# Paired products for B and C of two Mamba groups, and an earlier place for convolutions and two output copies

## The chip, the cores and the metric

The kernel runs on one core of a Trainium2 chip. The metric is the device time of one launch in microseconds (us). Engines are named as the profile names them: PE is TensorE's matmul, PEld its weight load, DVE VectorE, ACT ScalarE, POOL GpSimd, SP SyncE, which here only issues loads.

## What is computed

One decoder layer on 512 tokens with 16 learned meta tokens in front (length 528, width 1024), all in float32:

```python
u = rmsnorm(h, mix_norm_w)
proj = u @ w_in           # pool 1024, z 2048, xBC 4096, dt 32, two gates of 1024
xbc = silu(causal_depthwise_conv(xbc, conv_w, conv_b))          # width 4
y = ssd_chunked(x, dt, a, B, C) + x * d_skip    # 8 groups, 4 heads each of 64, state 128, chunks of 128
y = rmsnorm_per_group(y * silu(z)) * ssd_norm_w
y_ssd  = y @ w_ssd_out                           # 2048 -> 1024
y_pool = pool_mixer(proj's pool part) @ w_pool_up
h = h + (sigmoid(g0) * y_pool + sigmoid(g1) * y_ssd) @ w_o
h = h + relu(rmsnorm(h) @ w_ff1) ** 2 @ w_ff2    # hidden width 4096
out = rmsnorm(h)[meta tokens dropped]
```

Each of the eight groups of the state-space part needs a B and a C (128 channels each), an x of 256 channels (two tiles of 128) and a z of 256, all from w_in.

## The kernel before

**Products.** A float32 factor is split into a high and a low fp32r part: ACT casts the raw weight tile to `whi` (L111) and DVE subtracts it to `wlo` (L113). Each product is then three matmuls: high by high, high by low, low by high. `block` loads one weight tile of 128x1024 through SP and splits it with raised priority; `proj` (L215, L218) multiplies it with the eight row tiles of u, `uh` and `ul`.

**Scheduling.** The program is written as Python generators, and a scheduler orders each engine's instructions by dependencies, place in the program and priority. `tc.high_priority(100)` raises an instruction's priority, `tc.issue_after(x)` keeps an instruction behind another. Each engine takes its list in order.

**Scan stage.** For g from 0 to 7, `weave` (called at L933) steps in turn through `ssd(g)`, through `group_proj(g + 1)`, which makes the next group's inputs, and through side work: weight sums on POOL's queue (`weight_sums_at`) and, in the first four groups, sums of u. At g = 4 the first half of the output projection, `out_half` (eight products `pso`), comes ahead of the next group's projections. At g = 7 there is no next group; `out_part` (the products `psp` over the inputs 8 to 13) takes that place.

**`group_proj(g)`** makes B and C first, then x, for groups 2, 3 and 4 a gate (`pgp`), and z last (`pz`). A tile is made in one of two ways. `plain` multiplies one weight block: 48 matmuls in two column halves into a two-bank PSUM tile `px`, which `conv` reads directly. `pair` (L494 to L525) makes two tiles together with seven half-size products in place of eight: the left factors are quarters of the weight or sums of quarters, the right ones u, or sums of u's tiles made in the first four groups. `MULTIPLY` gives their order, b11, b21, t2, t1, s3, b22, t4; each has 12 matmuls of 264 columns. They go to two PSUM banks, `pq` and `po` (the first, third, fifth and seventh to `pq`); after each, the bank is copied by ACT (b11 L511, t2 L516, t1 L518, t4 L525) or added by DVE (b21 L513, s3 L521, b22 L523) into two raw tiles, `ra` and `rb` (`raw_pair`). The conv then reads those. Before the change x is made in this way for groups 4 to 7 (`X_PAIRS`), B and C for none (`BC_PAIRS` is empty). The weight sums are made by POOL's accumulating DMAs: each set of `fx` takes eight copies of 512 KB and serves two pairs; two sets are used before.

**`conv`** is ACT's Identity with scale and bias (L437), three DVE multiply-adds (L440) and ACT's Silu (L442), in the scheduler's ordinary priority.

**`ssd(g)`**: PE transposes B (`ptb`, L606), the meta part (`ptm`) and x (`ptx`, L619); DVE weights x (`xdt`, `xdd`); ACT makes two exponentials `eb` (L633), behind z's silu (L584) from group 4 on, eight Relu steps of the decay `abc` (L638, DVE does the other half at L641), and two exponentials over it (L644, L645). Then PE multiplies C with B (`pcb`, L656), DVE masks it, PE makes the chunks' states (`pst`, L663, L665), DVE passes them from chunk to chunk (L672, L673) and multiplies decay and mask (`dm`, L676). Two steps `po` (L685) and `py` (L691) give y; DVE multiplies it with z (L694 to L698); a norm over the group follows (`png` L709, L710). `filled` holds `pcb` behind the last matmul of the next group's first plain tile, `second_product` holds z's first matmul behind t2 of its group's x pair.

**The end of the scan.** `out_part` first multiplies inputs 8 to 11 for two output tiles (`psp0`, `psp1`), then inputs 12 and 13 for both together, kind of matmul by kind, and then copies both to `sp` (L868), from where POOL adds them into `acc_d` by DMA (L869); the other six output tiles follow. After the scan come the last inputs of the output projection, the pool branch (its products are at L998), gates, w_o and the MLP (lines from L940 on), none of which is edited.

Of the kernel before, what the change touches and what calls it, by code (L numbers as in the profile page):

```python
# [11 lines left out]
AF = mybir.ActivationFunctionType  # L12
ALU = mybir.AluOpType
# [3 lines left out]
SEQ = 512  # L17
# [17 lines left out]
V_MIX, V_BG, V_PS, V_CW, V_CB, V_DS, V_SN, V_MN, V_DTB, V_AL = (  # L35
    0, 8, 24, 32, 160, 192, 208, 224, 232, 233)
# [11 lines left out]
SUMS_AT = range(4)  # L48

X_PAIRS = (4, 5, 6, 7)  # L50
BC_PAIRS = ()
PAIRS = [(k, g) for g in range(G) for k in "bx" if g in (BC_PAIRS if k == "b" else X_PAIRS)]

SETS_AT = {0: 1, 1: 1, 2: 2, 3: 1, 4: 2, 5: 2, 6: 1, 7: 1}
# [10 lines left out]
def kernel(ctx: ExitStack, tc, xT, x, w, fx, f1, f2, vec, fnw, out):  # L65
    nc = tc.nc
    act, dve, pe, pool = nc.scalar, nc.vector, nc.tensor, nc.gpsimd
# [98 lines left out]
    def col(off, i, n=P):  # L166
        return vs[:n, off + i : off + i + 1]
# [25 lines left out]
    def psum2(name):  # L193
        return psa.tile([P, 1024], F32, tag="mm", name=name)
# [239 lines left out]
    def conv(dst, src, ct):  # L434
        n = dst.shape[-1]
        e = src.shape[-1] - n
        act.activation(dst, src[:, e:], AF.Identity, bias=col(V_CB, ct), scale=col(V_CW, ct * 4 + 3))  # L437
        for j in range(1, 4):
            o = max(0, j - e)
            dve.scalar_tensor_tensor(dst[:, o:], src[:, e + o - j : e + n - j],  # L440
                                     col(V_CW, ct * 4 + 3 - j), dst[:, o:], op0=ALU.mult, op1=ALU.add)
        silu = act.activation(dst, dst, AF.Silu)  # L442
        mark[0] = dst[:, :1]
        if ct < 16:
            x_ready[ct // 2] = silu
# [48 lines left out]
    def pair(kind, g, r):  # L494

        banks = (psum2(f"pq{kind}{g}")[:, :HALF], psum1(f"po{kind}{g}")[:, :HALF])
        operands = pair_operands(PAIRS.index((kind, g)))
        one, two = HF
        for m, f, n, start, stop in MULTIPLY:
            o = banks[n]  # L500
            wt = next(operands)
            f = factor_u(f)
            for low in range(2):
                for k in range(4):
                    wk = wt[low][:, k * P : (k + 1) * P]
                    at = pe.matmul(o, wk, f[k][0], start=start and not low and k == 0,  # L506
                                   stop=stop and low == 1 and k == 3, skip_group_check=True)
                    if not low:
                        pe.matmul(o, wk, f[k][1], start=False, stop=False, skip_group_check=True)
            if m == "b11":  # L510
                act.copy(r[0][:, one], o)  # L511
            elif m == "b21":
                dve.tensor_tensor(r[0][:, one], r[0][:, one], o, op=ALU.add)  # L513
            elif m == "t2":
                second_product[g] = at
                act.activation(r[1][:, one], o, AF.Copy, scale=-1.0)  # L516
            elif m == "t1":
                act.copy(r[1][:, two], o)  # L518
                yield
            elif m == "s3":  # L520
                dve.tensor_tensor(r[1][:, two], r[1][:, two], o, op=ALU.subtract)  # L521
            elif m == "b22":
                dve.tensor_tensor(r[1][:, one], r[1][:, one], o, op=ALU.add)  # L523
            else:
                act.copy(r[0][:, two], o)  # L525

    def raw_pair(kind, g):
        return [stg.tile([P, L], F32, tag=t, name=f"{t}{kind}{g}") for t in ("ra", "rb")]

    def group_proj(g, cur, gate=None):  # L530

        first = g == 0
        xc, bt, ct, zt = cur

        def plain(dst, t, skip):
            if first and (dst is bt or dst is ct):
                view = viewB if dst is bt else viewC
            else:
                runs, view = wide(psum2(f"px{g}_{t}"), skip)
                proj(runs, block(), X if first else U)  # L540
            conv(dst, first_raw(t, view, skip) if first else view, t)

        def z_half(ps, i):

            with tc.issue_after(done[0].ins) if g == 1 else nullcontext():
                wt = block(None, halved.get(g - 1) if gate is not None else None)
            proj(narrow(ps), wt, X if first else U, None if i else second_product.get(g))

        bcs = ((bt, 16 + g, 0), (ct, 24 + g, NM - 4))
        xs = ((xc[:, 0, :], 2 * g, 0), (xc[:, 1, :], 2 * g + 1, 0))  # L550
        both = g in BC_PAIRS
        for kind, ts, paired in (("b", bcs, both), ("x", xs, g in X_PAIRS)):
            if paired:
                r = raw_pair(kind, g)
                yield from pair(kind, g, r)
                for (dst, t, skip), src in zip(ts, r):
                    conv(dst, src[:, skip:], t)
                yield
            else:
                for t in ts:  # L560
                    plain(*t)
                    filled.setdefault(g - 1, mm[0])
                    yield
            if both:
                i = 0 if kind == "b" else 1
                ps = psum2(f"pz{g}_{i}")[:, :SEQ]
                z_half(ps, i)
                z_ready[g] = act.activation(zt[:, i, :], ps, AF.Silu)
                yield
        if both:  # L570
            return
        if gate is not None:
            gate_pool(gate)
            yield
        ps = psum2(f"pz{g}")
        for i in range(2):
            z_half(ps[:, i * SEQ : (i + 1) * SEQ], i)
        zf = zt.rearrange("p i t -> p (i t)")
        if first:
            dve.tensor_tensor(zt, ps.rearrange("p (i t) -> p i t", i=2),  # L580
                              rsb[:, NM:].unsqueeze(1).to_broadcast([P, 2, SEQ]), op=ALU.mult)
            z_ready[g] = act.activation(zf, zf, AF.Silu)
        else:
            z_ready[g] = act.activation(zf, ps, AF.Silu)  # L584
        yield
# [253 lines left out]
    def out_part():  # L839

        def get(n):
            t = block_tiles()
            block_load(t, slice(0, 1024))

            with after(b_meta[G - 1] if n == 1 else None):
                cast = act.copy(t[2], t[1])
            if n == 1:
                late_cast[0] = cast
            with tc.issue_after(x_decayed[G - 1].ins) if n == 1 else nullcontext():
                dve.tensor_tensor(t[3], t[1], t[2].bitcast(F32), op=ALU.subtract)  # L850
            return t

        def pieces():
            blocks = [get(0), get(1)]
            for n in range(6):
                t = blocks[n] if n < 2 else get(n)
                for j in range(NK):
                    c = slice(j * P, (j + 1) * P)
                    yield t[2][:, c], t[3][:, c]

        un = pieces()

        def part(ps, d, ks):
            mm3s(ps, [(next(un), ys[k]) for k in ks], ks[0] == 8, ks[-1] == 13)

        def add(ps, d):
            o = staged(f"sp{d}")
            act.copy(o, ps)  # L868
            nc.gpsimd.dma_start(acc_d[d], o, accum_op=ALU.add)  # L869


        ps = [psum2(f"psp{d}")[:, :SEQ] for d in range(2)]
        for d in range(2):
            part(ps[d], d, range(8, 12))
            yield
        late = [[(next(un), ys[k]) for k in (12, 13)] for d in range(2)]
        for o in ((0, 0), (1, 0), (0, 1)):
            for d in range(2):
                for n, (a, b) in enumerate(late[d]):
                    pe.matmul(ps[d], a[o[0]], b[o[1]], start=False, stop=o[1] == 1 and n == 1)  # L880
            yield
        for d in range(2):
            add(ps[d], d)
        for d in range(2, NK):
            ps = psum2(f"psp{d}")[:, :SEQ]
            part(ps, d, range(8, 14))
            add(ps, d)
            yield
# [791 lines left out]
def _weight_blocks(i):  # L1680
# [14 lines left out]

    def group(g, gate_d=None):
        z = lambda j: put(cols(w_in, OFF_Z + (2 * g + j) * P))
        both = g in BC_PAIRS
        for i, ts in enumerate(((16 + g, 24 + g), (2 * g, 2 * g + 1))):
            if g not in (X_PAIRS if i else BC_PAIRS):  # L1700
                for t in ts:
                    put(cols(w_in, OFF_XBC + t * P))
            if both:
                z(i)
        if gate_d is not None:
            gate(gate_d)
        if not both:
            for j in range(2):
                z(j)

    def wg(b):
        put(w_g[2 * b : 2 * b + 2].reshape(2, 2, P, 256).transpose(2, 0, 1, 3).reshape(P, 1024))
# [119 lines left out]
```

## Time and profile before

| | |
|---|---|
| device time, median of 3 runs | 1002.07 us (1002.04 to 1004.28) |
| the profiled execution | 1003.26 us |
| its span | 1001.6 us (1.66 us lie around it) |
| granted TensorE clock, mean | 0.999 |
| instructions | 15673 |
| moved by DMA | 184.52 MB; HBM read 173.13 MB, written 58.59 MB |

The busy times of the engines are shown with the prediction. In the span's 40 slices PE is at 9 tenths or more in all but the last, where it is at 7. The profile's chain that ended last goes over PE for 84%, DVE for 7%, ACT for 4% and DMA for 3%. The costliest groups are PE's matmuls and the two halves of the splits; the share of the loads' 16 DMA engines is 33.3% for SP's queue and 26.4% for POOL's.

A row of a view by time gives the start, the duration, engine, line and what is written from what; `x8` means eight instructions in one row, and what stands in brackets is the idle time ahead of it on its engine and what ended it. All times are in us from the start of the span.

### The profile page before, as it was taken

What the parts mean: (1) busy time and instruction counts of PE and PEld (TensorE: products, weight loads), DVE (VectorE), ACT (ScalarE), POOL (GpSimd) and SP (SyncE); (2) the same over time, 40 slices, a digit from 0 to 9 for tenths busy, and PEclk for the clock granted to TensorE, in tenths of its full rate; (3) what the DMA queues carried; (4) which work ended last, traced back from release to release, by engine and by line L of the source; (5) the groups of instructions that cost most, each with busy time, mean ns of one, the idle gap of its engine ahead of it and who ended that gap; (6) DMA issues with size and microseconds to landing.
All of it is one profiled execution on the core that took longest, in us unless ns stands there. A gap on an engine that the chain in (4) does not pass through costs nothing.

```text
span 1001.6 us, 15673 instructions
## 1 busy us (share of the span) xinstructions
PE 989.0 (99%) x6035; PEld 873.4 (87%) x6035; DVE 804.2 (80%) x1162; ACT 602.9 (60%) x855; POOL 121.9 (12%) x215
## 2 busy tenths in 40 slices
PE   9999999999999999999999999999999999999997
PEld 7889898989889999978898888888889999999986
DVE  7977997879855888978789667876988878888885
ACT  7657749494924658574345443377666666656654
POOL 0010321211212312223200001121000000000000
PEclk9999999999999999999999999999999999999999
DMA  7374868676798849678823732889354464454332
GB/s 245 89 254 140 265 182 238 195 192 199 221 262 265 232 122 278 211 161 172 286 68 127 252 101 77 259 232 323 88 197 149 142 194 138 157 185 151 129 106 84
DMA packets 61803, 184.52 MB, mean 184 GB/s; under 512 B 7072, under 2 KB 8416, under 8 KB 60704
## 3 DMA queue, kind: packets, MB, share of 16 engines
q1 hardware_dynamic: 39456, 109.00, 33.3%
q0 software_dynamic: 18240, 67.51, 26.4%
q10 hardware_dynamic: 4032, 7.00, 1.9%
q8 instruction: 47, 0.77, 0.3%
q14 instruction: 28, 0.23, 0.1%
HBM read 173.13 MB, written 58.59 MB: 231 GB/s over the span
## 4 chain that ended last, share of the span: by engine, by line
PE 84%; DVE 7%; ACT 4%; DMA 3%; issue 1%; SPq 0%; ACTq 0%; DVEq 0%
PE px L1451 8%; PE px L215 7%; PE alpha L1519 6%; PE pz L215 6%; PE px L1454 4%; PE px L218 4%; PE pgp L215 3%; PE alpha L1522 3%; PE pz L218 3%; PE pgs L215 3%; DMA raw<-in_w 2%; PE pqx L506 2%; PE py L691 2%; PE pgp L218 2%; PE pso L146 1%; PE wo_alpha L1213 1%
## 5 line engine op out<-in xcount | busy, mean ns | idle before, releaser
L113 DVE TENSOR_TENSOR wlo<-raw,whi 128x1024 fp32r<-128x1024 f32 (+2 forms) x88 | 102.2, 1171 | 45.0 <-ACT whi L111 29.7
L111 ACT CAST whi<-raw 128x1024 fp32r<-128x1024 f32 (+2 forms) x88 | 87.2, 1012 | 64.0 <-DMA raw<-in_w 15.8
L215 PE MATMUL px<-uh,whi 128*128 128x264 f32 (+1 forms) x320 | 81.1, 291 | 0.0
L218 PE MATMUL px<-ul,whi 128*128 128x264 f32 (+1 forms) x320 | 78.7, 284 | 0.0
L1226 DVE TENSOR_TENSOR ht<-ht,alpha 128x1024 f32<-128x1024 f32 x35 | 42.7, 1220 | 29.1 <-PE alpha L1519 29.1
L215 PEld LDWEIGHTS px<-uh,whi 128*128 128x128 f32 x320 | 60.5, 189 | 1.1 <-issue 0.9
L1149 ACT CAST shi<-rawf 128x1024 fp32r<-128x1024 f32 x42 | 44.2, 1053 | 28.0 <-PE alpha L1522 18.4
L218 PEld LDWEIGHTS px<-ul,whi 128*128 128x128 f32 x320 | 60.2, 188 | 0.4 <-issue 0.2
L1519 PE MATMUL alpha<-shi,hh 128*128 128x512 f32 x140 | 55.3, 395 | 0.7 <-DVE ht L1226 0.6
L1522 PE MATMUL alpha<-shi,hl 128*128 128x512 f32 x140 | 54.7, 391 | 0.0
L1150 DVE TENSOR_TENSOR slo<-rawf,shi 128x1024 fp32r<-128x1024 f32 x42 | 51.2, 1219 | 0.6 <-ACT shi L1149 0.6
L1454 PE MATMUL px<-vsl,shi 128*128 128x256 f32 x192 | 47.4, 280 | 0.0
L1451 PE MATMUL px<-vsh,shi 128*128 128x256 f32 x192 | 47.4, 281 | 0.0
L215 PE MATMUL pz<-uh,whi 128*128 128x512 f32 x112 | 43.8, 391 | 1.7 <-DVE xc L440 1.7
L218 PE MATMUL pz<-ul,whi 128*128 128x512 f32 x112 | 43.6, 390 | 0.0
L215 PE MATMUL px<-uh,wlo 128*128 128x264 f32 (+1 forms) x320 | 42.0, 283 | 0.0
L215 PEld LDWEIGHTS px<-uh,wlo 128*128 128x128 f32 x320 | 40.0, 188 | 0.0
L1519 PE MATMUL alpha<-slo,hh 128*128 128x512 f32 x140 | 37.4, 389 | 0.0
L1451 PEld LDWEIGHTS px<-vsh,shi 128*128 128x128 f32 x192 | 36.2, 188 | 0.9
L1454 PEld LDWEIGHTS px<-vsl,shi 128*128 128x128 f32 x192 | 36.1, 188 | 0.9
L1454 PE MATMUL px<-vl,shi 128*128 128x256 f32 x144 | 36.1, 283 | 0.0
L1451 PE MATMUL px<-vh,shi 128*128 128x256 f32 x144 | 36.0, 282 | 0.0
(599 smaller groups left out, 3068.3 us busy)
## 6 DMA issues: line engine op xcount, KB each, us to landing
raw<-in_w SPq DMA_DIRECT2D x96, 512.0 KB, 4.6
f_t<-in_f POOLq DMA_DIRECT2D x38, 512.0 KB, 7.5
f_s<-in_f POOLq DMA_DIRECT2D x26, 512.0 KB, 7.0
b<-in_f SPq DMA_DIRECT2D x21, 512.0 KB, 4.4
rawf<-in_f SPq DMA_DIRECT2D x36, 256.0 KB, 3.0
rawf<-f_t SPq DMA_DIRECT2D x36, 256.0 KB, 3.1
abc<-acs_d POOLq DMA_DIRECT2D x8, 1024.0 KB, 8.3
f_t<-f_t POOLq DMA_DIRECT2D x12, 512.0 KB, 6.7
```

Of the source, the lines that this page charges most:

```text
L111: act.copy(hi[:, c], raw[:, c])
L113: dve.tensor_tensor(lo[:, c], raw[:, c], hi[:, c].bitcast(F32), op=ALU.subtract)
L215: pe.matmul(o, wt, rhs[0][k][:, c], start=part == 0 and k == 0, stop=part == 1 and k == NK - 1)
L218: mm[0] = pe.matmul(o, wt, rhs[1][k][:, c], start=False, stop=False)
L506: at = pe.matmul(o, wk, f[k][0], start=start and not low and k == 0, stop=stop and low == 1 and k == 3, skip_group_check=True)
L1149: splits.append((act.copy(hi, src), dve.tensor_tensor(lo, src, hi.bitcast(F32), op=ALU.subtract)))
L1150: dve.tensor_tensor(lo, src, hi.bitcast(F32), op=ALU.subtract)))
L1226: added[0] = dve.tensor_tensor(o, o, src, op=op)
L1451: pe.matmul(ps, m, f[k][0], start=start and not low and k == 0, stop=stop and low == 1 and k == 3, skip_group_check=True)
L1454: pe.matmul(ps, m, f[k][1], start=False, stop=False, skip_group_check=True)
L1519: pe.matmul(ps[t], hh[:, p, seg, st], m, start=bool(first and not low and p == 0), stop=bool(last and low and p == 1), skip_group_check=True)
L1522: pe.matmul(ps[t], hl[:, p, seg, st], m, start=False, stop=False, skip_group_check=True)
```

## The change

1. `BC_PAIRS` becomes (5, 6): B and C of groups 5 and 6 are made by `pair` instead of two `plain` tiles. A third set of `fx` sums is made for them. Their raw values are held in the group's own x tile `xc` (128 x 2 x 528), which x's convolution overwrites later, and not in `ra` and `rb`.
2. For these groups z stays one step after x; an older form, in which half of z followed each pair, is taken out, here and in the order of the weight blocks. `filled` is set for them too: `pcb` of the group before stands behind the last matmul of the B and C pair's t2.
3. In `conv` the Identity and the three multiply-adds get raised priority; the Silu does not.
4. In `out_part` the inputs 12 and 13 are multiplied for one output tile after the other, and each tile's copy and its accumulating DMA follow at once with raised priority.

```diff
-BC_PAIRS = ()
+BC_PAIRS = (5, 6)
@@ def conv(dst, src, ct):
-        act.activation(dst, src[:, e:], AF.Identity, bias=col(V_CB, ct), scale=col(V_CW, ct * 4 + 3))
-        for j in range(1, 4):
-            o = max(0, j - e)
-            dve.scalar_tensor_tensor(dst[:, o:], src[:, e + o - j : e + n - j],
-                                     col(V_CW, ct * 4 + 3 - j), dst[:, o:], op0=ALU.mult, op1=ALU.add)
+        with tc.high_priority(100):
+            act.activation(dst, src[:, e:], AF.Identity, bias=col(V_CB, ct), scale=col(V_CW, ct * 4 + 3))
+            for j in range(1, 4):
+                o = max(0, j - e)
+                dve.scalar_tensor_tensor(dst[:, o:], src[:, e + o - j : e + n - j],
+                                         col(V_CW, ct * 4 + 3 - j), dst[:, o:], op0=ALU.mult, op1=ALU.add)
         silu = act.activation(dst, dst, AF.Silu)
@@ def group_proj(g, cur, gate=None):
-        both = g in BC_PAIRS
-        for kind, ts, paired in (("b", bcs, both), ("x", xs, g in X_PAIRS)):
+        for kind, ts, paired in (("b", bcs, g in BC_PAIRS), ("x", xs, g in X_PAIRS)):
             if paired:
-                r = raw_pair(kind, g)
-                yield from pair(kind, g, r)
+                r = raw_pair(kind, g) if kind == "x" else [xc[:, i, :] for i in range(2)]
+                for _ in pair(kind, g, r):
+                    filled.setdefault(g - 1, second_product[g])
+                    yield
                 for (dst, t, skip), src in zip(ts, r):
                     conv(dst, src[:, skip:], t)
                 yield
...
-            if both:
-                i = 0 if kind == "b" else 1
-                ps = psum2(f"pz{g}_{i}")[:, :SEQ]
-                z_half(ps, i)
-                z_ready[g] = act.activation(zt[:, i, :], ps, AF.Silu)
-                yield
-        if both:
-            return
@@ def out_part():
-        for o in ((0, 0), (1, 0), (0, 1)):
-            for d in range(2):
+        for d in range(2):
+            for o in ((0, 0), (1, 0), (0, 1)):
                 for n, (a, b) in enumerate(late[d]):
                     pe.matmul(ps[d], a[o[0]], b[o[1]], start=False, stop=o[1] == 1 and n == 1)
+            with tc.high_priority(100):
+                add(ps[d], d)
             yield
-        for d in range(2):
-            add(ps[d], d)
```

The order of the weight blocks loses the same two branches on `both`, and the plain B and C blocks of groups 5 and 6.

More of the change, by code (lines that the diff above doesn't have):

```diff
@@ L1697, in group @@
         z = lambda j: put(cols(w_in, OFF_Z + (2 * g + j) * P))
-        both = g in BC_PAIRS
         for i, ts in enumerate(((16 + g, 24 + g), (2 * g, 2 * g + 1))):
@@ L1702, in group @@
                     put(cols(w_in, OFF_XBC + t * P))
-            if both:
-                z(i)
         if gate_d is not None:
             gate(gate_d)
-        if not both:
-            for j in range(2):
-                z(j)
+        for j in range(2):
+            z(j)
     def wg(b):
```

## The prediction

> **What bounds the kernel now.** I read the page first (busy times), then the windows by stage, then the chain of waits around the two changed groups, and last the timelines of single engines where the new order puts a wait.
>
> ```profile
> PE 989.0 (99%) x6035; PEld 873.4 (87%) x6035; DVE 804.2 (80%) x1162; ACT 602.9 (60%) x855; POOL 121.9 (12%) x215
> ```
> ```profile
> 318.00:345.00 27.00, 27.00 (x190) 25.24 (x189) 22.76 (x30) 18.13 (x24) 7.24 (x10) 1.00 0.84 232
> 345.00:388.00 43.00, 42.91 (x315) 39.73 (x314) 33.70 (x53) 27.69 (x40) 8.55 (x16) 1.00 0.67 200
> 388.00:430.00 42.00, 41.97 (x308) 38.66 (x307) 36.85 (x59) 26.94 (x40) 10.59 (x20) 1.00 0.72 205
> 430.00:475.00 45.00, 43.33 (x228) 35.26 (x227) 38.35 (x59) 29.25 (x42) 12.16 (x18) 1.00 0.77 167
> ```
> After the stretch come its length and the busy time of PE, weight loads, DVE, ACT and POOL, then granted clock, DMA share and GB/s. PE is busy for all of it except 1.67 us in the last stretch, at full clock: TensorE bounds the scan stage. So a matmul removed shortens the run by its time, and any wait that PE meets lengthens it; DVE at 0.78 to 0.88 and ACT at 0.63 to 0.67 have room on average, but the order inside a stage decides.
>
> **The change part by part.** First the matmuls. The chain of waits gives plain B and C of group 5 and, right behind, its x pair:
>
> ```profile
> 312.16 1.81 PE pso L149 x8
> ...
> 319.81 0.23 PE png L709
> 320.04 0.23 PE png L710
> ...
> 324.06 1.92 PE px L215 x16
> ...
> 334.73 0.23 PE pz L215
> 334.96 0.23 PE pz L218
> ...
> 336.22 0.48 PE pqx L506 x4
> ```
> B and C run from 313.97 (312.16 + 1.81) to 325.98 (324.06 + 1.92), less two png of 0.23: 11.55 us for 96 matmuls. The x pair runs from there to 336.70, less two pz: 10.26 us for 84 (0.122 each). A pair in place of a plain B and C saves 1.29 us; two groups save 2.6.
>
> What a pair adds beside PE: seven half tiles to split instead of four, and seven copies or additions out of PSUM.
>
> ```profile
> L113 DVE TENSOR_TENSOR wlo<-raw,whi 128x1024 fp32r<-128x1024 f32 (+2 forms) x88 | 102.2, 1171 | 45.0 <-ACT whi L111 29.7
> 366.81 0.38 ACT L511 COPY rax<-pqx 128x264 f32<-128x264 f32 x1 [2.61 <-PE pqx L506]
> ```
> DVE gets 1.5 splits of 1.17 and three additions, taken at the copy's 0.38 for the same 128x264: about 2.9 us a group; ACT four copies, 1.5, and as many casts. In 345 to 388 DVE goes from 33.70 to 36.6 of 41.7, still under PE, so this costs nothing as work: PE's own matmuls cover it. Were PE 5 us shorter there, it would not. SP loads 768 KB more a group, at DMA shares of 0.84 and 0.67: nothing.
>
> Group 5's pair (while group 4's scan ends) stands behind eight projections of the output's half; ACT's long exponentials of group 4 are far past. In the new program's order 14 pz matmuls stand between the x pair's second and third steps, which covers the copies that wait behind the prioritized convolutions. I take 0.2 us, between 0 and 1.
>
> Group 6's pair is another matter. It now stands right behind pz of group 5, with group 5's transposes, and the same pz releases ACT's longest run of work:
>
> ```profile
> 345.32 1.82 PE pz L215 x8
> ...
> 347.80 0.87 PE ptx L619 x8
> ```
> ```profile
> 347.18 1.03 ACT L584 ACTIVATE zt<-pz 128x1024 f32<-128x1024 f32 x1 [0.77 <-PE pz L215]
> ...
> 348.70 1.28 ACT L633 ACT_TABLE_LOAD   x1
> 349.99 2.14 ACT L633 ACTIVATE eb<-abc 64x1024 f32<-64x1024 f32 x2
> ...
> 355.47 1.04 ACT L644 ACTIVATE abc<-abc 128x1024 f32<-128x1024 f32 x1
> 356.41 0.78 ACT L437 ACTIVATE bt<-px,vs 128x528 f32<-128x528 f32 x1
> ```
> ```profile
> 382.73 0.65 ACT L442 ACTIVATE xc<-xc 128x528 f32<-128x528 f32 x1 [0.38 <-DVE xc L440]
> ```
> The pair's third product (t2) accumulates onto the bank of its first (b11), which ACT must copy out first (L511). In the new order of ACT that copy stands behind zt, a silu, btok, the table load, both eb, eight L638, L645 and L644. Before, 9.23 us pass from zt's start (347.18) to the instruction after L644 (356.41), and only a convolution waited there, hidden behind the plain C. Now: 347.18 + 9.23 + silu 0.65 + copy 0.38 = 357.44, or 10.3 us after pz ends at 347.14. PE has until then the transposes (to 348.67, 1.53 us) and 24 products of 0.122 (2.9): 4.5 us. PE waits 5.8 us, with t2, t1, pcb, pst and everything later queued behind, none of which it can take first. On ACT the casts of group 6's x pair are queued behind the copy, and wait as well. Bounds: 4.5 if PE's waits inside the transposes take part of it, 7 if DVE holds L645 up.
>
> The priority of the convolutions frees PSUM earlier. One PE wait of the scan's start goes:
>
> ```profile
> 104.23 0.76 DVE L440 SCALAR_TENSOR_TENSOR xc<-px,vs,xc 128x525 f32<-128x525 f32 x1
> ```
> ```profile
> 105.13 0.47 PE L215 MATMUL pz<-uh,whi 128*128 128x512 f32 x1 [1.69 <-DVE xc L440]
> ```
> In the new order that convolution stands before the group's y steps and splits, some 5 us earlier, well before PE's 103.44. I take 1.7 saved; next late are the splits of pz's weights, which stand behind and still come before pz's low part. The end on the other side is 0.
>
> In group 6's scan the priority costs something. B's convolution of group 7 now takes its silu between the two exponentials, so two table loads and a silu (1.28 + 0.65 + 1.28) delay the second:
>
> ```profile
> 403.53 2.29 DVE L676 TENSOR_TENSOR abc<-abc,cbm 128x2048 f32<-128x2048 f32 x1
> ```
> ```profile
> 405.92 1.09 PE L691 MATMUL py<-abc,xdt 128*64 128x128 f32 x16
> ```
> L676 and py come about 3 us later, but the new PE order has 16 pair matmuls ahead of py. Only the pair's t2, behind a copy that waits for the late exponential, stops PE: I take 0.5, between 0 and 2.5. "ScalarE: Activation LUTs", section "What ACT_TABLE_LOAD costs", of the Trainium skill puts a switch at about 2.66 us, a drain of 1.38 included. By the rows above, a load at 348.70 is followed by the first exponential at 349.99, 1.29 us and no drain; by the page the two switches would be 2.8 us longer and the sum 4.1 us, not 1.3.
>
> The copies of the output's middle part:
>
> ```profile
> 442.58 1.06 ACT L644 ACTIVATE abc<-abc 128x1024 f32<-128x1024 f32 x1
> ...
> 444.49 1.05 ACT L645 ACTIVATE abc<-abc 128x1024 f32<-128x1024 f32 x1
> 445.44 1.05 ACT L868 COPY sp<-psp 128x512 f32<-128x512 f32 x2
> ```
> ```profile
> 446.06 0.50 PE L146 MATMUL psp<-yh,whi 128*128 128x512 f32 x1 [1.44 <-ACT sp L868]
> ```
> The first half's last matmuls now come together, its copy stands right behind L644 (443.6), and it is done at about 444.1 while PE is still in the second half's (to 444.4). 1.4 us saved; 0 at worst.
>
> POOL gets one more set of weight sums (eight copies of 512 KB), which pushes the later sets back. Group 7's scan holds eight copies instead of four, among the accumulations L869 and ahead of the loads L1043; none of these is near its user. The load that is near is SP's:
>
> ```profile
> 475.93 6.25 DMA raw<-in_w
> ```
> ```profile
> 483.66 0.39 PE L998 MATMUL pz<-t1h,whiB 128*128 128x264 f32 x1 [0.40 <-ACT pu L1010]
> ```
> ACT's copy stood behind a cast that waited for it, and 0.4 us reached PE. More traffic may add to it: 0.5, between -0.4 and 2.
>
> **Sum.** Saved 2.6 + 1.7 + 1.4 = 5.7; added 5.8 + 0.2 + 0.5 + 0.5 = 7.0. The profiled execution took 1003.26 us (span 1001.6 and 1.66 around it), so it would take 1004.6. It is 1.2 above the median of the runs, 1002.07; for them I forecast 1003.4. This kernel's runs tell 0.3% (3 us) from no change.
>
> **The rivals.** *The wait at group 6's pair does not form* (ACT's copy runs ahead, or PE finds other work). Then all savings stay: 1.3 - 5.8 = -4.5, 997.6 for the runs. For it speaks that everything else is covered; against it, that both engines take their lists in order and that nothing of the pair is free of that bank.
>
> *DVE becomes a second wait behind ACT's.* Six convolution steps of B and C (0.76 each, 4.6 us) now stand among group 5's state updates, ahead of the last, which po needs. Laid out from pcb's end by the rows, that update is done 0.5 us before PE asks. If DVE is later than that, PE pays up to 4.6 - 0.5 = 4.1 more: 1007.5. For it speaks DVE's share of 0.88; against it, that DVE rests while PE waits for ACT.
>
> *The early savings do not come*, since the new orders only swap one wait for another at pz and at psp: 1.3 + 3.1, or 1006.5. *Table switches cost the longer price*: 1.3 + 2.8, or 1006.2; the row of 1.29 us speaks against it.
>
> **How the numbers follow.** Forecast, two groups of savings against one wait: 0.57. No wait at the pair: 0.13. DVE: 0.18. Savings absent: 0.10. Long switches: 0.02. The forecast's own range is 1000.5 to 1005.5. Faster by over 3 us: the first rival and the forecast's lower edge, 0.15; slower: the three others less their near ends, 0.27; within: 0.58. The range goes from 999.0, halfway between the forecast's own lower end (wait at 4.5, nothing for groups 5 and 6, -0.4 for the DMA) and the first rival, to 1007.5, the second rival, and leaves out most of the first.
>
> **What would show it.** Right: a PE wait of 5 to 6 us behind the first 24 products of group 6's pair, ended by the ACT copy L511; no idle PE at the first pz or at psp's third block; 24 fewer PE matmuls. Wrong: that wait under 3 us, or a DVE state update or a raw load as the longest new releaser of PE.

## The result: 1.3% slower

| | median of the runs | lowest to highest |
|---|---|---|
| before | 1002.79 us | 1002.04 to 1004.28 |
| after | 1015.57 us | 1014.21 to 1018.67 |

The ratio of after to before is 1.0126, 95% interval 1.0107 to 1.0145. The forecast was 1003.4 in a range from 999.0 to 1007.5: the time is 8 us above its upper end. The profiled execution of after took 1016.59 us with a span of 1014.9, 13.3 above the span of before (1001.6).

The page's first part and the view of PE's waits, of after:

```profile
PE 991.8 (98%) x6011; PEld 875.1 (86%) x6011; DVE 809.7 (80%) x1172; ACT 611.0 (60%) x869; POOL 131.7 (13%) x227
```
```profile
PE pqb L507 <- ACT xc L512: 5.5, 1, 5.5
PE png L703 <- ACT qhg L330: 3.0, 1, 3.0
PE pxx L992 <- ACT pu L998: 2.7, 1, 2.7
PE pz L992 <- ACT pu L1004: 2.3, 1, 2.3
...
PE po L679 <- DVE st L667: 1.2, 2, 0.9
```

A row names the waiting line, what ended the wait, the time in sum, how often and the longest. The same view of before:

```profile
PE pz L215 <- DVE xc L440: 1.7, 1, 1.7
...
PE psp L146 <- ACT sp L868: 1.4, 1, 1.4
PE alpha L1519 <- DVE ht L1226: 0.6, 1, 0.6
PE pz L998 <- ACT pu L1010: 0.4, 1, 0.4
```

Three readings. The two waits that were to go (pz, psp) are gone. The wait that was to come is there, at pqb, with 5.5 us and the releaser that was named (L511 of before is L512 of after). Beside it stand waits that the prediction did not have: 3.0 at png, and 5.0 in two pieces at the first products after the scan, `pool_pair` (L992; L998 of before). And PE is busy 2.8 us longer (991.8 against 989.0) with 24 matmuls fewer. PE's idle time in the span grew by 10.5 (from 12.6 to 23.1), and 10.5 + 2.8 are the 13.3.

PE is busy longer because its granted clock falls. The windows of after around the wait at pqb (after the stretch and its length: busy time of PE, weight loads, DVE, ACT, POOL; then clock, DMA share, GB/s):

```profile
351.00:357.60 6.60, 1.13 (x10) 0.91 (x8) 2.84 (x10) 6.55 (x14) 1.53 (x4) 0.91 0.79 254
357.60:360.40 2.80, 2.76 (x12) 2.76 (x13) 1.66 (x2) 0.93 (x1) 0.00 (x0) 0.50 0.01 3
360.40:363.00 2.60, 2.60 (x14) 2.60 (x13) 0.00 (x0) 0.94 (x2) 0.00 (x0) 0.50 0.67 202
363.00:366.00 3.00, 3.00 (x20) 2.79 (x19) 2.28 (x4) 1.14 (x3) 0.00 (x0) 0.95 0.18 11
```

The wait ends at 357.64, and t2 and t1 run at a clock of 0.50 until 363.29: they take 5.65 us instead of 2.9, so the wait of 5.5 costs 8.2. Removed matmuls (2.6) and a busy time that is 2.8 longer make 5.4 us of slow matmuls in all. "TensorE: Matmul & The Clock Gate", section "Part 1: The HAM clock gate (the "warmup" mystery)", of the Trainium skill says that the clock halves after an idle window of about 3.4 us, counted by a window that runs freely. That fits the wait of 5.5; the last section has shorter waits.

### The profile page after: what moved, and what is told of

The parts are those of the page before. It is cut to its first block, busy times and chain, and to the rows that moved or that the text cites. A ratio compares the mean times of both kernels' runs of the same rounds, so it can differ in the third digit from the quotient of the medians.

```text
span 1014.9 us, 15682 instructions
## 1 busy us (share of the span) xinstructions
PE 991.8 (98%) x6011; PEld 875.1 (86%) x6011; DVE 809.7 (80%) x1172; ACT 611.0 (60%) x869; POOL 131.7 (13%) x227
## 4 chain that ended last, share of the span: by engine, by line
PE 87%; ACT 4%; DVE 4%; DMA 3%; issue 1%; POOL 0%; SPq 0%; ACTq 0%; POOLq 0%; DVEq 0%
PE px L1445 8%; PE alpha L1513 6%; PE px L215 6%; PE pz L215 5%; PE px L1448 4%; PE alpha L1516 3%; PE px L218 3%; PE pgp L215 3%; PE pz L218 3%; PE pgs L215 3%; PE py L685 2%; PE pqx L507 2%; PE pso L146 1%; PE po L679 1%; PE wo_alpha L1207 1%; PE pf L147 1%
## 5 line engine op out<-in xcount | busy, mean ns | idle before, releaser
L113 DVE TENSOR_TENSOR wlo<-raw,whi 128x1024 fp32r<-128x1024 f32 (+2 forms) x84 | 97.3, 1168 | 38.3 <-ACT whi L111 28.7
L111 ACT CAST whi<-raw 128x1024 fp32r<-128x1024 f32 (+2 forms) x84 | 83.3, 1008 | 57.0 <-DMA raw<-in_w 16.2
L215 PE MATMUL px<-uh,whi 128*128 128x264 f32 (+1 forms) x256 | 65.1, 292 | 0.0
L218 PE MATMUL px<-ul,whi 128*128 128x264 f32 (+1 forms) x256 | 63.4, 285 | 0.0
L215 PEld LDWEIGHTS px<-uh,whi 128*128 128x128 f32 x256 | 48.3, 189 | 0.8 <-issue 0.7
L218 PEld LDWEIGHTS px<-ul,whi 128*128 128x128 f32 x256 | 48.2, 188 | 0.2
L113 DVE TENSOR_TENSOR wlop<-rawp,whip 128x1024 fp32r<-128x1024 f32 (+1 forms) x24 | 26.1, 1087 | 23.3 <-ACT whip L111 9.9
L111 ACT CAST whip<-rawp 128x1024 fp32r<-128x1024 f32 (+1 forms) x24 | 22.3, 939 | 20.3 <-PE pso L147 11.7
```

The source lines that it names most:

```text
L111: act.copy(hi[:, c], raw[:, c])
L113: dve.tensor_tensor(lo[:, c], raw[:, c], hi[:, c].bitcast(F32), op=ALU.subtract)
L215: pe.matmul(o, wt, rhs[0][k][:, c], start=part == 0 and k == 0, stop=part == 1 and k == NK - 1)
L218: mm[0] = pe.matmul(o, wt, rhs[1][k][:, c], start=False, stop=False)
```

## The experiments

The theory after this comparison: three separate causes (the copy of b11 behind ACT's exponentials; the convolutions' priority ahead of group 1's norm; POOL's later weight sums at the pool pair), and a half clock after each long wait. Times are medians; "against before" is the ratio to the runs of the kernel before that were made beside it, with its interval.

**The parts alone.** First the pairs, with `conv` and `out_part` as before:

> The change with the convolutions and the two output copies as before: only B and C of groups 5 and 6 as pairs, with the third set of weight sums. Theory (three causes: the copy of b11 behind ACT's exponentials, the conv's priority ahead of group 1's norm, POOL's later weight sums ahead of the accumulations; and TensorE's clock at half for some us after each wait over 2.5 us): the wait at t2 of group 6's pair stays (about 5.5, and 2.5 for the slow matmuls behind it), the waits at the pool pair stay (5.0, and 1.5), the wait of 3.0 at png is gone, matmuls -2.6; together about 12 above before, 1014. Rival (the waits at the pool pair come from the delayed y steps of group 7, an effect of the conv's priority): those go as well, and it is about 1008.

1011.44 us, 1.0088 (1.0073 to 1.0103) against before. The t2 wait is 5.5; at the pool pair 1.8 and 0.2 are left of the 5.0, and png's 3.0 is gone. So the pairs alone lose 8.7 of the 12.8, and 3 of the 5 us at the pool pair come only with the other edits. The theory's 1014 was 2.6 too high, since it left the pool pair its full 5.0.

Then the priority of `conv`, without anything else:

```diff
-        act.activation(dst, src[:, e:], AF.Identity, ...)
+        with tc.high_priority(100):
+            act.activation(dst, src[:, e:], AF.Identity, ...)   # and the three multiply-adds
```

> The kernel before with only the conv's priority. Theory: the first pz wait of 1.7 goes, the wait of 3.0 at png of group 1 comes with 2 us of half clock behind it: about 3 us slower than before, 1005.5, and no wait at t2 (it is a plain tile here) and none over 1 us at the pool pair. Rival (priority harms only beside the pairs, since group 6's casts and copies make the queue): no png wait, 1000.5.

1005.75 us, 1.0035 (1.0023 to 1.0047): as the theory had it. The first pz wait is gone and png's 3.0 is there. ACT's timeline of after shows how; of group 1's norm, sqg and qhg are steps:

```profile
150.40 0.65 ACT L443 ACTIVATE xc<-xc 128x528 f32<-128x528 f32 x1 [3.49 <-DVE xc L441]
150.95 1.05 ACT L697 ACTIVATE sqg<-yt 128x1024 f32<-128x1024 f32 x1
152.02 1.28 ACT L750 ACT_TABLE_LOAD   x1
153.31 0.69 ACT L750 ACTIVATE gp<-pgp,vs 128x512 f32<-128x512 f32 x1
153.90 0.61 ACT L330 CAST qhg<-sqg 128x512 fp32r<-128x512 f32 x1
```

Six convolution steps of group 2's x stand between group 1's y steps on DVE, sqg starts at 150.95 (149.16 before), and while DVE adds its halves ACT takes a gate's table load and sigmoid, which before came behind qhg (151.49). PE reaches png first, and waits until 154.56.

The new order of the output's middle part alone:

> The kernel before with only the new order of the output's middle part. Theory of two shares at the pool pair (the edit lets TensorE run 1.4 ahead of DVE's and ACT's chain over group 7's norm, and puts ACT's copies ahead of that chain's casts; the late accumulations on POOL's queue take the rest of the room): the psp wait of 1.4 goes, the room ahead of the pool pair shrinks from 5.4 us to about 2 and no wait over 1 us comes yet: 1000.7 to 1002.7. Rival (the edit alone makes the waits of 2.7 and 2.3): 1006.

1007.87 us, 1.0045 (1.0029 to 1.0061). The rival was right: this edit, forecast as 1.4 saved, costs 4.5. The three parts alone lose 8.7, 3.05 and 4.5, more together than the whole change with its 12.8: their losses at the pool pair do not add up. psp's wait is gone, and these are there:

```profile
PE pz L998 <- ACT pu L1010: 3.7, 1, 3.7
...
PE pxx L998 <- ACT pu L1004: 1.2, 1, 1.2
```

**What ends the waits at the pool pair.** The chain of waits of before, and of this kernel (other pieces left out):

```profile
474.38 0.24 PE psp L147
...
474.68 1.23 DVE wloD L133
...
475.93 6.25 DMA raw<-in_w
...
482.28 1.05 ACT whi L111
483.33 0.29 ACT pu L1010
```
```profile
470.07 0.59 ACT sp L868
470.66 0.53 ACT yh L721
...
471.21 1.29 DVE yl L722 x2
...
474.82 0.28 ACT sp L868
...
475.30 1.06 ACT whiD L132
...
476.39 1.24 DVE wloD L133
...
477.64 7.40 DMA raw<-in_w
...
485.14 1.04 ACT whi L111
486.18 0.29 ACT pu L1010
```

The load of the next weight block is issued when wloD has read the raw tile, in both kernels. In before wloD starts when two things are through at nearly the same time: a chain over DVE and ACT from group 7's scan (y, norm, yh, yl, the sums sm, the split wloS), and psp, whose product ahead of it ends at 474.62. The view of the chain takes the way over psp. In before PE came to the end of this load only 0.4 us early. Without psp's wait PE starts the pool pair at 473.9 instead of 475.8 and then waits for the same load. Moreover ACT's later copies sp now stand ahead of the casts that the other chain needs (470.07 ahead of yh, 474.82 ahead of whiD), each behind its psp; the load goes out at 477.64 instead of 475.93 and lands after 7.40 us, not 6.25. Two runs for the shares of this:

> The changed kernel with the output's middle part in its old order. Theory: the waits at the pool pair fall from 5.0 in sum to under 2.5, the half clock there goes, and the psp wait of 1.4 comes back; waits at t2 (5.5) and png (3.0) stay: about 3.5 below the changed kernel, 1012. Rival (the conv's priority is what delays group 7): the waits at the pool pair stay at 5, 1016.

1016.55 us: no better than after. The waits at the pool pair fall to 2.0, but psp's 1.4 is back, and the half clock still follows the last of them. PE's earlier place ahead of the pool pair is not the only thing that sets its end.

> The changed kernel with no set of weight sums in group 7's scan (the set is made later, behind the loads of the residual). Theory: ACT's wait for the staging tile of the output's middle part goes, and with it the waits of 2.7 and 2.3 at the pool pair and the half clock behind the first: 6 below the changed kernel, 1009.5. Rival (group 7's y steps are late by themselves): the waits stay over 2 us, 1014 to 1016.

1015.67 us: the same as after. ACT's wait for the staging tile is gone (5.0 us in after, ended by `acc_d<-sp`), but the copy then waits for psp instead, and the waits at the pool pair are 1.2 and 3.2. The sums alone don't explain them. Counted from group 7's pcb, the load goes out after 37.6 us in before, 40.9 in after, 40.5 with the output's old order (the run ahead of this one), and 39.4 without the sums: the new order and the added sums each delay it, so taking out one of them leaves the other's delay.

```diff
-            act.copy(o, ps)
+            with after(halved[G - 1] if d == 4 else yh_cast[0] if d == 6 else None): act.copy(o, ps)
```

> The kernel before with the new order of the output's middle part, and with ACT's copies of the fifth and the seventh output tile held behind the casts of group 7's norm (qhg and yh), so that ACT takes these casts first, as before the change. Theory (the edit alone costs 4.5 since ACT's later copies, each waiting for psp, come ahead of these casts and make the pool pair's sums late; TensorE's lead of 1.4 is harmless): the waits of 1.2 and 3.7 at the pool pair fall under 1 and the psp wait stays gone: 1002, or about 1 under before. Rival (TensorE's lead by itself uses up the room): waits over 3 stay, 1006.

1006.98 us, 1.0034 (1.0022 to 1.0047): the theory fell. ACT takes the casts first, the wait of 1.2 is gone, and one of 5.3 takes the place of 3.7. The chain shows the load again:

```profile
473.65 0.59 ACT sp L868
474.24 0.95 ACT whiD L132
...
475.22 1.24 DVE wloD L133
...
476.47 8.60 DMA raw<-in_w
...
485.15 1.05 ACT whi L111
```

It goes out 0.5 later than in before (1.0 later when counted from group 7's pcb) and takes 8.60. The two held copies did not give ACT its whole old order back: the last copy sp, released by psp, still stands ahead of the cast whiD, for which wloD waits (in before it stands behind, at 476.05). So this run doesn't tell TensorE's lead from ACT's order. While PE waits, the clock falls to 0.50. Whether POOL's eight loads of acc beside it make it slow was to be seen next:

> The kernel with the output's new order and the two held copies, and POOL's eight loads of acc (256 KB each) held behind the pool pair's copy of its fourth product, so that they do not run beside SP's raw load for the pool pair. Theory (that load, issued at 476.5 and landing 8.6 later instead of 6.3, is late because POOL's loads of acc are issued in one block at 472.8 to 477.8): the load takes 6 or less, the wait of 5.3 falls to 2 or less and its half clock goes: 1001 to 1003. Rival (the load takes as long by itself, and TensorE's lead of 2.4 is lost anyway): the wait stays over 4, 1007.

> The kernel before with the loads of acc held in the same way: the control. Theory: the raw load lands sooner, pz's wait of 0.4 goes, nothing else: 1002 to 1003, the same as before. Rival: the sums over acc become late and cost over 2: 1005.

1006.65 and 1002.41 us; but the edit didn't move the loads (the first is issued at 472.28 in the one, at 472.77 without the edit), so this stays open. The second has the order of before, and its time is the same within the interval (0.9999, 0.9988 to 1.0009). But its profiled execution is the slowest of its eleven, 1006.77 us: there the raw load took 7.95 and the wait for it was 2.1. The load's own time differs by 1.7 us between executions of the same order.

**Mending the pairs.** ACT's copies of a pair at raised priority:

```diff
-                act.copy(r[0][:, one], o)
+                with tc.high_priority(100): act.copy(r[0][:, one], o)     # and the other three
```

> The changed kernel with ACT's four copies of each pair at raised priority, so that b11's copy goes ahead of the second exponential of group 5 (its new place on ACT: behind the first eb). Theory: the wait at t2 falls from 5.5 to about 2 (two eb and the table load, less the first 24 products), its half clock goes; about 6 below the changed kernel, 1009.5, with the waits at png and the pool pair still there. Rival (DVE's state updates take over as the wait): 1013 or more.

1011.42 us, 4.2 below after. The wait at t2 is gone altogether, with its half clock; in its place group 5's norm waits for 2.1 and 0.4. That takes 2.5 of the 8.2 back, and the pool pair, reached sooner, takes 18.9 (477.60 to psl at 496.54) where after takes 17.2.

> The kernel before with the conv's priority for the two x tiles of group 1 alone. Theory: the pz wait of 1.7 at about 104 goes and the png wait of 3.0 does not come, since the convolutions of group 2's x stay behind group 1's y steps: 1.7 faster than before, 1001. Rival (png's wait comes from the steps of group 1 that are moved, too): 1004 or more.

1002.39 us, 0.9994 (0.9983 to 1.0005): no png wait, but no gain either. The wait for the same convolution moves from pz (105.13, 1.7) to the x product ahead of it:

```profile
PE px L215 <- DVE xc L441: 1.7, 1, 1.7
```

> B and C of groups 5 and 6 as pairs, with ACT's four copies of each pair at raised priority, the conv's priority for group 1's x alone and the output's middle part in its old order. Theory: no wait at t2 of group 6's pair, none at png of group 1, under 2 at the pool pair, so that the 2.6 of matmuls and the 1.7 of pz are left against about 2 to 3 of waits at group 5's norm and the pool pair: 1000 to 1003. Rival (DVE's extra work around the pairs and POOL's sums cost more by themselves): 1006 or more.

1007.61 us, 1.0043 (1.0031 to 1.0056). No wait at t2 or png, and still slower: 1.7 at group 6's transposes (ptx at 392.19), ended by DVE, and 1.8 at the pool pair with the half clock behind it.

> The kernel of the last set (both pairs, their copies first, conv priority for group 1's x, output in its old order) without the set of weight sums in group 7. Theory: with the output's old order the eight copies of POOL in group 7 are what keeps a staging tile late and costs 1.8 of wait and 1.5 of half clock at the pool pair; without them 3 less than that kernel, 1004.5. Rival (it is the later loads of the pool pair's weights by themselves): no change, 1007.5.

1005.02 us, 1.0014 (0.9999 to 1.0028): with the output's old order the weight sums do cost, 2.6 here. Both pairs together, with the causes found so far taken away, come to the time of before within the interval, and no lower. Its profile has 0.7 at group 5's norm, 0.7 at group 6's transposes and 0.6 at group 6's py.

> The changed kernel mended: both pairs with their copies first, no priority for convolutions, the output's new order with the two copies held, no weight sums in group 7. Theory: -2.6 and -1.4, against 1.7 at group 5's transposes and up to 2 of half clock there: 1000 to 1002. Rival: 1005 or more, with a wait that stands in none of the kernels so far.

1007.95 us, the rival's time, but with no new wait: the 3.3 at the pool pair are those of the output's new order.

> The mended change (both pairs with their copies first, no priority for convolutions, the output's new order with held copies, no weight sums in group 7) with the loads of acc held as well. Theory: its wait of 3.3 at the pool pair and the half clock behind it go: 5 less than without, 1003. Rival: 1007 or more.

1006.92 us, the same, since here too the loads of acc stayed in place.

> B and C of group 5 alone as a pair, no priority for convolutions, the output's new order with the two copies held, no weight sums in group 7. Theory: matmuls -1.3, psp -1.4, no wait at group 6, none over 1 at the pool pair: 1000. Rival (one pair already makes DVE late for group 5's transposes, or the moved set of sums costs later): 1004.

1009.44 us, with 4.4 at the pool pair for the same reason.

**One pair alone.** Group 5's B and C, with `conv` and output as before and no sums in group 7:

> The kernel before with B and C of group 5 alone as a pair, convolutions and the output's middle part as before, and no weight sums in group 7. Theory (the wait at t2 belongs to group 6's pair, the wait at png to the conv's priority, the long waits at the pool pair to the output's new order and the sums): none of them is there, and of the 1.3 of matmuls what group 6's y steps leave stays: 1001.5 to 1003, at most 0.1% under before. Rival (a pair of B and C costs by its own copies and splits wherever it stands): 1004 or more.

1007.07 us, 1.0047 (1.0033 to 1.0061): a loss, in runs from 1005.1 to 1009.1. Its profiled execution (1005.53 us, the second shortest) shows where the gain goes. Group 6's pcb starts at 395.38, 1.06 earlier than before (396.44). Then:

```profile
PE py L684 <- issue: 1.3, 1, 1.3
PE po L678 <- DVE st L666: 1.1, 1, 1.1
```

DVE's timeline of this kernel has the mask that py needs at

```profile
405.09 2.28 DVE L669 TENSOR_TENSOR abc<-abc,cbm 128x2048 f32<-128x2048 f32 x1
```

and before had it at 403.53. The cause of the first row is read from this order; the view itself names only "issue". By group 7's pcb PE's lead of 1.1 has become a lag of 1.6.

DVE is not late by its own work. Ahead of the mask it waits 2.9 us for ACT's cast yh, and ACT has waited before. Its copy of B's transposes, in before and in this kernel, and POOL's queue in this kernel:

```profile
391.48 0.58 ACT L608 COPY btok<-ptb 128x512 f32<-128x512 f32 x1
```
```profile
393.00 0.59 ACT L601 COPY btok<-ptb 128x512 f32<-128x512 f32 x1 [2.46 <-POOL seen L790]
```
```profile
390.40 0.84 POOL L776 DMA_DIRECT2D f_t<-f_t  x1 [7.48 <-DMA f_t<-in_f]
...
392.23 0.73 POOL L790 COPY seen<-qhg 128x1 f32<-128x1 f32 x2
```

`seen` is a copy of one column with which the kernel marks, on POOL's queue, how far the scan has come before it issues the next copy of weight sums. Here it reads qhg of group 5's norm, which lies in the buffer that btok of group 6 overwrites, so btok has to wait for it. POOL takes it late, behind a copy of weight sums (of a set that before makes in group 4's scan) that waited 7.48 us for an earlier one to land; in before the last such `seen` ends at 388.17, 3.3 us ahead of btok. Up to btok the steps of ACT move with PE's lead (zt at 387.52, 388.56 in before), so up to there no tie with DVE or ACT takes the lead away. The same wait stands in every kernel with a pair of B and C whose copies are not put first, in no other one, and PE's waits in group 6's scan grow with it (us, one execution each):

| kernel | ACT ahead of btok | PE at po and py |
|---|---|---|
| after, without sums in group 7 | 0.9 | 0.8 |
| after, output in its old order | 1.1 | 1.0 |
| after | 1.3 | 1.2 |
| pairs only | 1.6 | 1.5 |
| group 5's pair, output's new order | 1.8 | 1.7 |
| group 5's pair alone | 2.5 | 2.4 |

No run takes this wait alone away, so its price in the medians is not shown. Why the other executions of this kernel take up to 3.6 us more than the profiled one stays open; the two longest have a mean clock of 0.995 and 0.996, the profiled one 0.999.

## Why the prediction was wrong

The largest term, the wait at t2, came as it was worked out. Four other steps failed: POOL's later weight sums were put at nothing, the conv's priority was costed at one of its calls, psp's removed wait was taken for a gain, and the clock was left out.

- **Matmuls, -2.6: right in size.** 24 fewer. Across group 5's pair (from pso to the next ptb) after gains 1.1 on before, 1.29 less the 0.2 that was taken for it.
- **POOL's weight sums, 0 outside the DMA term: the step that failed is "none of these is near its user".** The prediction looked for the price of the later sets in group 7 alone. In group 5's scan they make POOL late for a marker copy that ACT's btok waits for: 1.3 us in after, and 2.5 in the last experiment, where it takes the whole lead of the removed matmuls. In group 7 they delay the pool pair's load; taken out of the kernel with the output's old order they give 2.6 back.
- **The wait at group 6's pair, +5.8: right.** 5.5, with the copy behind zt, the table load, eb, and L638, L645 and L644 (lines of before). ACT's timeline of after, for the working in the prediction (it gave 357.44 for the copy's end):

```profile
356.29 1.04 ACT L638 ACTIVATE abc<-abc 128x1024 f32<-128x1024 f32 x1
357.23 0.35 ACT L512 COPY xc<-pqb 128x264 f32<-128x264 f32 x1
```

- **The clock: not in the sum at all.** Every row of before that the prediction read has the clock at 1.00, with no wait of PE over 1.7; from these it took a microsecond of waiting for a microsecond of time. The wait of 5.5 cost 2.7 more, all waits together 5.4: with the 2.7 the forecast would have been 1006.1. The page of the Trainium skill named above has the clock halve after an idle window, and the prediction did not weigh that.
- **The first pz wait, -1.7: the wait went, the price was elsewhere.** It checked that the splits of pz's weights stood behind and were in time, for group 1's x alone. The same priority acts in each group, and in group 2 it puts six steps into the y steps of group 1. That cost 3.0 and half clock behind it; alone the edit costs 3.05 in the median. The rival on the early savings had the sign, no gain at all, but not a loss.
- **psp, -1.4: wrong in sign.** Alone it costs 4.5. The prediction quoted the load at 475.93 with 6.25 and the wait of 0.4 behind it, and charged them to traffic at 0.5. The step that failed is that PE's earlier end is a gain. The prediction didn't follow the chain back from that load to wloD, where the chain from group 7's norm ends together with psp: by the rows of before whiS could start about 0.6 us earlier without psp's copy (sm ends at 471.85, whiS starts at 472.46), an estimate of the most that an earlier psp could gain at wloD. And it didn't ask where ACT's later copies sp would come to stand: ahead of that chain's casts, so that the load goes out 1.9 later, counted from group 7's pcb.
- **Group 6's scan, 0.5 between 0 and 2.5:** about 2.0 (after's lag on before at ptb grows from 7.7 at group 6 to 9.7 at group 7), inside the bounds, but mostly by luck: t2's wait behind the late exponential, the mechanism that was forecast, is 0.5 (`pqx` behind `rax`, the same in the kernel with the priority alone), and 1.2 are the waits at po behind btok and POOL.
- **DMA at 475 to 483, 0.5 between -0.4 and 2: mis-sized.** The pool pair takes 17.2 us in after (483.76 to psl at 500.99) against 10.9 (475.81 to 486.68).
- **The rival of DVE as a second wait** put it at po of group 5. There is none over 1 us there; in group 6 it is 1.2 in two pieces, and DVE is late there because of btok.

So on the spot the three savings came about as they were priced (24 matmuls, the waits at pz and psp), and so did the wait at t2; the losses came elsewhere. Missing from the sum are 4.1 at the pool pair (5.0 less before's 0.4 and the 0.5 taken), 3.0 at png, 1.5 in group 6's scan and 5.4 of slow clock, 14.0 together; between the sum (1004.6) and the profiled execution (1016.59) lie 12.0. Of the 2.0 between them, 0.6 is before's wait at alpha, which is not in after's view, and 0.3 the wait at t2, shorter than forecast; the rest is not settled.

## What to carry to other kernels

A PE that is 99% busy can still be level with another chain: before counting a removed wait as gain, follow the next waits downstream, however small, back to what started their releaser, and see whether the removed work is on that way. A priority given to a helper acts at each of its calls, so it is to be costed at each place where it can pass something, not only where it helps. A copy that only marks progress holds a buffer too, and passes the lateness of its queue on to whoever overwrites it. In these runs a wait of PE cost its length and, in some executions, half clock behind it.

## What the runs showed of the hardware

The half clock follows shorter waits than expected, and not each time. In the profiled executions of all 18 kernels the granted clock is either 1.00 or 0.50, and it changes only on a grid of 3.41 us: ahead of the last microseconds 15 stretches of half clock last 3.41 us and 8 last 6.83, and the stretches at full clock between them are whole multiples of 3.41. Where the grid lies against the program differs from execution to execution. The same png wait of 3.0 us falls into one step of it in the kernel with the conv's priority alone, and is shared by two in the one with the copies first:

```profile
151.17:154.59 3.42, 0.40 (x2) 0.00 (x0) 0.69 (x2) 3.39 (x5) 2.14 (x4) 1.00 0.48 69
154.59:158.00 3.41, 3.39 (x11) 2.74 (x12) 3.05 (x3) 3.38 (x4) 2.11 (x3) 0.50 1.04 174
```
```profile
150.54:153.95 3.41, 1.67 (x8) 1.06 (x6) 1.76 (x3) 2.83 (x3) 1.94 (x4) 1.00 0.83 280
153.95:157.37 3.42, 2.11 (x12) 1.77 (x13) 1.88 (x3) 3.39 (x6) 2.32 (x4) 1.00 0.94 162
157.37:160.78 3.41, 3.41 (x17) 2.81 (x15) 2.82 (x4) 3.40 (x5) 0.07 (x1) 1.00 1.03 266
```

PE was busy for 0.40 of 3.42 us ahead of the half clock, and for 1.67 and 2.11 in the two steps that no half clock followed. The psp wait of 1.4 us shows how near the limit it can be, in before and in the kernel with priority for group 1's x alone:

```profile
442.27:445.68 3.41, 2.13 (x10) 1.27 (x8) 3.41 (x11) 3.41 (x6) 0.00 (x0) 1.00 0.34 133
```
```profile
443.15:446.56 3.41, 1.98 (x10) 1.03 (x8) 3.41 (x6) 3.41 (x5) 0.80 (x2) 1.00 0.01 5
446.56:449.97 3.41, 3.41 (x21) 2.86 (x21) 3.41 (x6) 1.28 (x2) 1.02 (x2) 0.50 0.88 108
```

The first was followed by full clock. Over the 18 executions, half clock followed each of the 21 steps at full clock in which PE was busy for less than 0.48 of the time, 2 of the 15 between 0.48 and 0.59 (0.52 and 0.58), and none above. So a busy share within one step decides here, and not the length of a wait.

That the same wait does both fits the free-running window of the page named above of the Trainium skill ("TensorE: Matmul & The Clock Gate", Part 1), and so does the step of 3.41 us; that a whole window has to be idle does not fit steps in which PE was busy for 0.4 to 0.58 of the time and half clock followed. One step of half clock costs 1.7 us of matmuls where PE is busy throughout, half of its length. In the runs of before beside the experiments, 45 with a mean clock of 0.999 took 1002.4 us on average and 21 with 0.997 took 1004.1, which suits one such step in the latter; no trace of theirs shows it.
